# A hybrid decoder layer on one core: the attention stage with TensorE's instructions in a written-out order

## The chip, the core and the metric

The kernel runs on one core of a Trainium2 chip. A core has five engines with an instruction stream each: TensorE (PE in the profile; its weight loads are shown as PEld), VectorE (DVE), ScalarE (ACT), GpSimd (POOL) and SyncE (SP), which here only issues transfers. Each stream is fixed when the kernel is built; an engine takes its instructions in that order, and an instruction whose semaphore isn't set yet holds up all that stand behind it on its engine. Matmuls write to PSUM, eight banks of 128 x 512 floats; everything else lives in SBUF. The metric is the time of one execution on the device in microseconds (us), the median of the runs.

## The reference, cut to what matters

One decoder layer on x of 512 tokens x 1024, in float32:

```
proj = x @ w_in                       # q, k, v, forget logits, z, xBC, dt, two gates
log_f = log_sigmoid(f_logit + b_forget)
attn: 16 heads of 64; logit[t,s] = q_t.k_s / 8 + sum_{s<j<=t} log_f_j, causal softmax, times v
ssm:  Mamba-2 SSD, 32 heads of 64 in 4 groups, state 128, chunks of 128, gated RMS norm
mixed = (g0 * (attn @ w_proj_attn) + g1 * (ssm @ w_proj_ssm)) @ w_out    # g = sigmoid(gate + b)
x = layer_norm(a * x + mixed)
x = layer_norm(a * x + (silu(x @ w_ffn_gate) * (x @ w_ffn_up)) @ w_ffn_down)
```

## The kernel before, in words

Every large product is made of three matmuls on operands that are split into a high and a low part (`mm3`, lines 135 to 137), each with up to 512 moving columns. A weight chunk of 128 x 1024 comes in by one transfer on SP's queue (`load_w`), and `split` makes its two parts: ScalarE copies the high one (line 101), VectorE subtracts the low one (line 102). There are four buffers for raw chunks and three for each part.

Two helpers make projections. `gemm_ws` holds weights still: 256 output rows in two PSUM banks (tag `gps`, four banks), eight weight blocks of 128, so 16 times `mm3` for the usual 1024 inner rows, or 48 matmuls; then `evac` empties each bank. `gemm_xs` holds the tokens still: 512 output columns in four `gps` banks, 32 times `mm3`.

The stages are: the transposed x; for four groups the SSD branch (`group_bc`, `group_x`, `group_z`, `group_y`, `group_u`, `group_proj`); attention; the two gate projections; the attention output projection; `w_out` and the first layer norm; a feed-forward part; the second layer norm.

In attention, `att_qk(hg, isq, qk)` projects q or k of four heads. Its evacuation makes two tiles per head: ScalarE copies (line 397), VectorE copies and subtracts (lines 398 and 399), GpSimd sets ones and issues a small transfer of the forget sums. These tiles have two buffers per tag, so those of one group of four heads come free as that group's scores are done. `att_v(hg)` projects v of eight heads. `att_head` then does one head:

- scores: for each of four query blocks two matmuls of 128, 256, 384 or 512 columns into one bank (tag `cps`, four banks; lines 426 and 427);
- softmax of each block: VectorE masks and takes the maximum (line 431), ScalarE takes the exponential (line 433), VectorE the reciprocal (line 434) and the scaling (line 435) of a tile `t_y`;
- ten 128 x 128 transposes (line 448) into three `cps` banks, each split by ScalarE and VectorE into high and low tiles (`t_uh`, `t_ul`, `t_sq`, `t_xw`);
- PV: eight matmuls into a `cps` bank (line 454), whose two halves ScalarE (line 458) and VectorE (line 459) add up.

The order on each engine is set when the kernel is built: a scheduler takes the instructions by the order in which the program writes them, with estimated times, and issues on each engine the first that is ready. So TensorE's order around a head is the scheduler's: the projections that are written later (the next group's q and k, then the second gate's `evac_g1`, lines 650 to 660) stand between the parts of a head as filler. Weight splits have a higher priority.

Of the kernel before, what the change touches and what calls it, by code (L numbers as in the profile page):

```python
# [1 line left out]

# [9 lines left out]
AF = mybir.ActivationFunctionType  # L13
ALU = mybir.AluOpType
# [4 lines left out]
T = 512  # L19
NT = T // P  # L20
# [20 lines left out]
def tile_hybrid_decoder_layer(  # L41
# [58 lines left out]
    def split(hi, lo, src):  # L100
        nc.scalar.copy(out=hi, in_=src)  # L101
        nc.vector.tensor_tensor(out=lo, in0=src, in1=hi.bitcast(F32), op=ALU.subtract)  # L102

    def gps():
        return psum.tile([P, T], F32, name="gps", bufs=4)

    def cps():
        return psum.tile([P, T], F32, name="cps", bufs=4)
# [7 lines left out]
    def slot(tag, shape=(P, T), dtype=F32):  # L116
        return HOME.get(tag, sbb).tile(list(shape), dtype, name="t_" + tag, tag=tag, bufs=BUFS[tag])

    def big(tag, a=4, dtype=F32):
        return slot(tag, (P, a, 2048 // a), dtype)  # L120
# [13 lines left out]
    def mm3(o, l, r, start, stop, skip=False):  # L134
        nc.tensor.matmul(out=o, lhsT=l[0], rhs=r[0], start=start, stop=False, skip_group_check=skip)  # L135
        nc.tensor.matmul(out=o, lhsT=l[0], rhs=r[1], start=False, stop=False, skip_group_check=skip)  # L136
        nc.tensor.matmul(out=o, lhsT=l[1], rhs=r[0], start=False, stop=stop, skip_group_check=skip)  # L137
# [1 line left out]
    def ws_chunk(w, c0, half, dst=None):  # L139
        return load_w(w[half * 512:(half + 1) * 512, c0:c0 + 256], 4, 256, dst)  # L140

    def gemm_ws(w, c0, nk, rhs, evac, alloc=gps, n=T, chunks=None):

        ps = [alloc()[:, 0:n] for _ in range(2)]
        for half in range(nk // 4):
            hi, lo = chunks[half] if chunks else ws_chunk(w, c0, half)
            for b in range(2):
                bs = slice(b * P, (b + 1) * P)
                for k in range(4):
                    kt = half * 4 + k  # L150
                    mm3(ps[b], (hi[k][:, bs], lo[k][:, bs]), rhs(kt), kt == 0, kt == nk - 1)
        for b in range(2):
            evac(b, ps[b])

    def gemm_xs(w, c0, lhs, evac, before=None):

        ps = [gps() for _ in range(NT)]
        for kc in range(KD // 2):
            hi, lo = load_w(w[kc * 256:(kc + 1) * 256, c0:c0 + T], 2, T)
            for tt in range(NT):  # L160
                if before is not None and kc == 0:
                    before(tt)
                for k in range(2):
                    kt = kc * 2 + k
                    mm3(ps[tt], lhs(kt, tt), (hi[k], lo[k]), kt == 0, kt == KD - 1)
                if kc == KD // 2 - 1:
                    evac(tt, ps[tt])

    def down_chunk(w, kc, half, dst=None):
        return load_w(w[kc * 256:(kc + 1) * 256, half * T:(half + 1) * T], 2, T, dst)  # L170
# [208 lines left out]
    QK = (("v", "th", "bT", "cT"), ("btok", "cbm", "xst", "xdt"))  # L379

    def att_qk(hg, isq, qk):
        c0 = (C_Q if isq else C_K) + hg * 256
        sc = 0.125 if isq else 1.0

        def evac(b, ps):
            for par in range(2):
                h = hg * 4 + 2 * b + par
                src = ps[par * 64:(par + 1) * 64, :]
                t1 = slot(QK[isq][2 * par], (68, T), F32R)
                t2 = slot(QK[isq][2 * par + 1], (P, T), F32R)  # L390
                a, l_ = (0, 64) if isq else (64, 0)
                nc.gpsimd.memset(t1[64:68, :].bitcast(F32), 1.0)
                if isq:
                    nc.gpsimd.dma_start(out=t1[64:66, :], in_=cuT[h:h + 33:32, :])
                else:
                    nc.gpsimd.dma_start(out=t1[66:68, :], in_=cuT[64 + h:97 + h:32, :])
                nc.scalar.activation(out=t1[0:64, :], in_=src, func=AF.Copy, scale=sc)
                nc.vector.tensor_copy(out=t2[a:a + 64, :], in_=t1[0:64, :].bitcast(F32))
                nc.vector.scalar_tensor_tensor(out=t2[l_:l_ + 64, :], in0=src, scalar=sc, in1=t1[0:64, :].bitcast(F32),
                                               op0=ALU.mult, op1=ALU.subtract)  # L400
                qk[(isq, h)] = (t1, t2)
        gemm_ws(w_in, c0, KD, rhs_x, evac)

    def att_v(hg):

        vt = [slot("xtok", (P, NT, 4, P), F32R) for _ in range(2)]

        def evac(tt, ps):
            sv = ps.rearrange("p (h d) -> p h d", h=8)
            for i in range(2):  # L410
                hi = vt[i][:, tt, :, 0:64]
                nc.scalar.copy(out=hi, in_=sv[:, 4 * i:4 * i + 4])
                nc.vector.tensor_tensor(out=vt[i][:, tt, :, 64:128], in0=sv[:, 4 * i:4 * i + 4], in1=hi.bitcast(F32), op=ALU.subtract)
        gemm_xs(w_in, C_V + hg * 256, lhs_x, evac)
        return vt

    def att_head(h, qk, vt, of):
        hh = h % 4
        q1, q2 = qk[(True, h)]
        k1, k2 = qk[(False, h)]  # L420
        pr = []
        for i in range(NT):
            n = (i + 1) * P
            qs = slice(i * P, (i + 1) * P)
            ps = cps()
            nc.tensor.matmul(out=ps[:, 0:n], lhsT=q1[:, qs], rhs=k1[:, 0:n], start=True, stop=False)  # L426
            nc.tensor.matmul(out=ps[:, 0:n], lhsT=q2[:, qs], rhs=k2[:, 0:n], start=False, stop=True)  # L427
            sm = cst0.tile([P, 3], F32, name="sm", bufs=6)
            pt = slot("y")

            nc.vector.tensor_tensor_reduce(out=pt[:, 0:n], in0=ps[:, 0:n], in1=mneg[:, T - n:T], scale=-1.0, scalar=-NEG,  # L431
                                           op0=ALU.add, op1=ALU.min, accum_out=sm[:, 2:3])
            nc.scalar.activation(out=pt[:, 0:n], in_=pt[:, 0:n], func=AF.Exp, scale=-1.0, bias=sm[:, 2:3], accum_out=sm[:, 0:1])  # L433
            nc.vector.reciprocal(out=sm[:, 1:2], in_=sm[:, 0:1])
            nc.vector.tensor_scalar(out=pt[:, 0:n], in0=pt[:, 0:n], scalar1=sm[:, 1:2], scalar2=None, op0=ALU.mult)
            pr.append(pt)
        ab = big("uh" if h % 2 == 0 else "ul", 4, F32R)
        cc = slot("sq" if h % 2 == 0 else "xw", (P, 2, 256), F32R)
        pT = {}
        for j, kbs in enumerate(((0,), (1, 3), (2,))):  # L440
            ps = cps()
            o = 0
            hi, lo = (ab[:, j, :], ab[:, 2 + j, :]) if j < 2 else (cc[:, 0, :], cc[:, 1, :])
            for kb in kbs:
                w = T - kb * P
                pT[kb] = (hi[:, o:o + w], lo[:, o:o + w])
                for i in range(kb, NT):
                    nc.tensor.transpose(out=ps[:, o:o + P], in_=pr[i][:, kb * P:(kb + 1) * P], identity=ident)  # L448
                    o += P
            split(hi[:, 0:o], lo[:, 0:o], ps[:, 0:o])  # L450
        po = cps()
        for kb in range(NT):
            for j in range(2):
                nc.tensor.matmul(out=po[:, kb * P:], lhsT=vt[:, kb, hh, :], rhs=pT[kb][j],  # L454
                                 start=kb == 0 and j == 0, stop=kb == NT - 1 and j == 1)
        rows = slice((h % 2) * 64, (h % 2 + 1) * 64)
        tb = slot("yo", (64, T))
        nc.scalar.copy(out=tb, in_=po[64:128, :])
        nc.vector.tensor_tensor(out=of[rows, :], in0=po[0:64, :], in1=tb, op=ALU.add)
# [152 lines left out]
    for g in range(NG):  # L612
# [10 lines left out]
        elif g < NG - 1:  # L623
            st = group_bc(g + 1)
            for pair in range(2):
                group_x(g + 1, st, pair)
    att_qk(0, True, qk)
    att_qk(0, False, qk)
    group_proj(NG - 1, u)


# [3 lines left out]
        oslots += [b_[:, i, :] for i in range(4)]  # L635
    oslots += [slot("ab", (P, T), F32R) for _ in range(6)]
    oT = [(oslots[2 * i], oslots[2 * i + 1]) for i in range(KD)]
    for hg in range(4):
        if hg > 0:
            att_qk(hg, True, qk)  # L640
            att_qk(hg, False, qk)
        if hg % 2 == 0:
            vts = att_v(hg)
        vt = vts[hg % 2]
        for h in range(4 * hg, 4 * hg + 4):
            if h % 2 == 0:
                of = slot("dx")
            att_head(h, qk, vt, of)
            if h % 2 == 1:
                split(oT[h // 2][0], oT[h // 2][1], of)  # L650


    for pair in range(4):
        def evac_g1(b, ps):
            j = 2 * pair + b
            th = slot("y")
            nc.scalar.activation(out=th, in_=ps, func=AF.Tanh, scale=0.5, bias=vec[:, 32 + j:33 + j])
            nc.vector.scalar_tensor_tensor(out=sd[j], in0=th, scalar=1.0, in1=sd[j], op0=ALU.add, op1=ALU.mult)
        gemm_ws(w_in, C_G + D + pair * 256, KD, rhs_x, evac_g1)
    g0 = {}  # L660
    for pair in range(4):
        def evac_g0(b, ps):
# [395 lines left out]
```

## Time and profile before

| | us |
|---|---|
| median of 3 runs (1150.43 to 1151.94) | 1150.79 |
| the profiled execution | 1153.12 |
| its span, first to last instruction | 1151.4 |
| TensorE busy in the span | 1121.1 (97%) |
| VectorE busy | 776.6 (67%) |
| ScalarE busy | 528.4 (46%) |
| GpSimd busy | 133.8 (12%) |

The profile's page gives the busy time of each engine and the span in 40 equal slices, a digit for the busy tenths of each slice. Other views ask the trace: windows (busy time of each engine in a stretch), the timeline (instructions in order of time: start, duration, engine, line, operation, output and inputs, shapes, count; idle time before it in brackets), waits (who waited for whom), and groups of instructions by line. Matmuls are pipelined and their ends are modelled; what one costs is read from the starts of neighbours. A few records of matmuls are missing. The attention stage lies from 461.7 us on, the first score matmul, to 644.5 us.

### The profile page before, as it was taken

Reading aid. Unit: us, or ns where it says so; the run is one execution under the profiler, and the core shown is the slowest. Engines: PE = TensorE matmul, PEld = TensorE weight load, DVE = VectorE, ACT = ScalarE, POOL = GpSimd, SP = SyncE. Lnnn points to the kernel's source line nnn. Section 1 sums busy time; section 2 is a strip of 40 time slices with the busy share of each in tenths; the row PEclk is TensorE's granted clock in tenths of the full one; section 3 lists DMA queues with packets and bytes.
Section 4 is the critical chain, followed back from the end, with each engine's and each line's share of the span. In section 5 each row is a group of like instructions: output and inputs, shape, how many; then the busy total and the mean of one; then the engine's idle time right before and its main releaser. Section 6 shows DMA issues by size and latency. Waiting matters only on the chain.

```text
span 1151.4 us, 15793 instructions
## 1 busy us (share of the span) xinstructions
PE 1121.1 (97%) x6086; PEld 942.4 (82%) x6086; DVE 776.6 (67%) x1219; ACT 528.4 (46%) x912; POOL 133.8 (12%) x165
## 2 busy tenths in 40 slices
PE   7999999999999999999999999999999999999996
PEld 5887778778787788777777888888999999988885
DVE  3679974884787563889598534556986877667326
ACT  3376664454542432666465444214654554452210
POOL 3003130030123100221110000020111111100001
PEclk9999999999999999999999999999999999999998
DMA  8343233233231233211212235381778786465211
GB/s 249 91 132 115 85 112 92 92 110 93 91 91 58 91 92 95 71 56 56 80 51 57 80 124 179 118 195 68 205 177 216 170 199 155 93 228 175 92 55 74
DMA packets 115772, 134.21 MB, mean 117 GB/s; under 512 B 5636, under 2 KB 93936, under 8 KB 115568
## 3 DMA queue, kind: packets, MB, share of 16 engines
q1 hardware_dynamic: 99328, 112.80, 31.6%
q0 software_dynamic: 14640, 14.10, 7.6%
q10 hardware_dynamic: 1728, 6.29, 1.5%
q8 instruction: 48, 0.79, 0.3%
q14 instruction: 28, 0.23, 0.1%
HBM read 128.78 MB, written 4.26 MB: 116 GB/s over the span
## 4 chain that ended last, share of the span: by engine, by line
PE 44%; DVE 3%; issue 3%; DMA 2%; ACT 1%; POOL 0%; DVEq 0%; POOLq 0%; ACTq 0%; SPq 0%
PE gps L135 9%; PE gps L136 9%; PE gps L137 9%; PE cps L136 5%; PE cps L137 5%; PE cps L135 5%; DMA rq<-in_w_ffn_up_dram 1%; PE cps L448 1%; PE cps L454 1%; DMA t_sd<-in_x_dram 0%; DVE xr L726 0%; PE cps L426 0%; DMA raw<-in_w_ffn_down_dram 0%; PE cps L427 0%; DVE wlo L102 0%
## 5 line engine op out<-in xcount | busy, mean ns | idle before, releaser
L102 DVE TENSOR_TENSOR wlo<-raw,whi 128x1024 fp32r<-128x1024 f32 x127 | 156.3, 1230 | 210.7 <-ACT whi L101 210.2
L101 ACT CAST whi<-raw 128x1024 fp32r<-128x1024 f32 x127 | 133.6, 1052 | 272.4 <-PE gps L137 109.5
L135 PE MATMUL gps<-xh,whi 128*128 128x512 f32 x456 | 181.6, 398 | 0.0
L136 PE MATMUL gps<-xl,whi 128*128 128x512 f32 x456 | 181.6, 398 | 0.0
L137 PE MATMUL gps<-xh,wlo 128*128 128x512 f32 x456 | 181.3, 398 | 0.0
L101 ACT CAST wh<-rq 128x1024 fp32r<-128x1024 f32 (+1 forms) x84 | 82.2, 980 | 101.0 <-PE cps L136 44.9
L102 DVE TENSOR_TENSOR wl<-rq,wh 128x1024 fp32r<-128x1024 f32 (+1 forms) x84 | 94.9, 1132 | 33.8 <-ACT wh L101 33.7
L135 PEld LDWEIGHTS gps<-xh,whi 128*128 128x128 f32 x456 | 86.2, 189 | 16.5 <-issue 0.2
L136 PEld LDWEIGHTS gps<-xl,whi 128*128 128x128 f32 x456 | 86.2, 189 | 16.1 <-issue 0.2
L137 PEld LDWEIGHTS gps<-xh,wlo 128*128 128x128 f32 x456 | 86.2, 189 | 15.5
L135 PE MATMUL gps<-whi,xh 128*128 128x512 f32 x192 | 76.2, 397 | 3.8 <-ACT xh L101 3.7
L137 PE MATMUL gps<-whi,xl 128*128 128x512 f32 x192 | 75.8, 395 | 0.0
L136 PE MATMUL gps<-wlo,xh 128*128 128x512 f32 x192 | 75.7, 394 | 0.0
L233 DVE SCALAR_TENSOR_TENSOR t_v<-gps,cw,t_v 128x511 f32<-128x511 f32 (+2 forms) x72 | 53.4, 744 | 3.9 <-ACT t_v L230 3.1
L136 PE MATMUL gps<-t_ul,whi 128*128 128x512 f32 x128 | 51.1, 399 | 0.0
L137 PE MATMUL gps<-t_uh,wlo 128*128 128x512 f32 x128 | 51.0, 399 | 0.0
L135 PE MATMUL gps<-t_uh,whi 128*128 128x512 f32 x128 | 50.5, 395 | 0.0
L135 PEld LDWEIGHTS gps<-whi,xh 128*128 128x128 f32 x192 | 36.6, 190 | 12.3 <-ACT xh L101 4.4
L433 ACT ACTIVATE t_y<-t_y,sm 128x128 f32<-128x128 f32 (+1 forms) x64 | 35.8, 561 | 19.3 <-DVE sm L431 17.7
L315 ACT ACTIVATE t_ab<-t_ab,acum 128x128 f32<-128x128 f32 x128 | 41.8, 393 | 4.9 <-DMA t_ab<-ac_d 4.7
L784 POOL DMA_DIRECT2D rq<-in_w_ffn_gate_dram x12 | 15.5, 1296 | 244.6 <-ACT xh L686 158.7
L136 PEld LDWEIGHTS gps<-wlo,xh 128*128 128x128 f32 x192 | 36.6, 191 | 8.0 <-DVE wlo L102 0.5
(567 smaller groups left out, 2762.0 us busy)
## 6 DMA issues: line engine op xcount, KB each, us to landing
raw<-in_w_in_dram SPq DMA_DIRECT2D x80, 512.0 KB, 3.6
rq<-in_w_ffn_gate_dram SPq DMA_DIRECT2D x25, 512.0 KB, 4.7
rq<-in_w_ffn_up_dram SPq DMA_DIRECT2D x25, 512.0 KB, 5.3
raw<-in_w_ffn_down_dram SPq DMA_DIRECT2D x22, 512.0 KB, 3.8
t_ab<-ac_d SPq DMA_DIRECT2D x32, 256.0 KB, 3.3
raw<-in_w_proj_ssm_dram SPq DMA_DIRECT2D x16, 512.0 KB, 3.4
rq<-in_w_ffn_gate_dram POOLq DMA_DIRECT2D x10, 512.0 KB, 7.0
rq<-in_w_ffn_up_dram POOLq DMA_DIRECT2D x10, 512.0 KB, 6.1
```

What stands on the lines that cost most here:

```text
L101: nc.scalar.copy(out=hi, in_=src)
L102: nc.vector.tensor_tensor(out=lo, in0=src, in1=hi.bitcast(F32), op=ALU.subtract)
L135: nc.tensor.matmul(out=o, lhsT=l[0], rhs=r[0], start=start, stop=False, skip_group_check=skip)
L136: nc.tensor.matmul(out=o, lhsT=l[0], rhs=r[1], start=False, stop=False, skip_group_check=skip)
L137: nc.tensor.matmul(out=o, lhsT=l[1], rhs=r[0], start=False, stop=stop, skip_group_check=skip)
L233: nc.vector.scalar_tensor_tensor(out=v[:, sh:], in0=ps[:, 0:T - sh], scalar=cw[:, k, blk:blk + 1], in1=v[:, sh:], op0=ALU.mult, op1=ALU.add)
L315: nc.scalar.activation(out=m[:, r, :], in_=m[:, r, :], func=AF.Relu, scale=-1.0, bias=acum[:, c, h:h + 1])
L433: nc.scalar.activation(out=pt[:, 0:n], in_=pt[:, 0:n], func=AF.Exp, scale=-1.0, bias=sm[:, 2:3], accum_out=sm[:, 0:1])
L448: nc.tensor.transpose(out=ps[:, o:o + P], in_=pr[i][:, kb * P:(kb + 1) * P], identity=ident)
L454: nc.tensor.matmul(out=po[:, kb * P:], lhsT=vt[:, kb, hh, :], rhs=pT[kb][j], start=kb == 0 and j == 0, stop=kb == NT - 1 and j == 1)
L784: nc.gpsimd.dma_start(out=self.v(t), in_=self.q(*s_), accum_op=ALU.add)
```

## The change

`gemm_ws` becomes a generator, `ws_steps`, that hands control back after each `mm3`; `gemm_ws` runs it to its end. The evacuation of a bank is now written right behind that bank's last matmul. `xs_steps` is the same for the v projection. `att_head` falls into three functions: `att_scores` (scores and softmax), `att_transposes`, `att_values` (PV). The main loop of attention is written inside `tc.manual_schedule(engines={PE})`: there TensorE's instructions stand in the order in which the program writes them; the other engines keep the scheduler. Head h is: some filler steps, PV of head h-1, the ten transposes of head h, some more filler, the scores of head h+1. `before_t` and `after_t` count the filler for each head. Through head 7 the filler is q and k of groups 1 and 2 (64 steps); then v of the upper eight heads (32 steps), q and k of group 3 (32) and the second gate (64). The second gate's tanh is written back into its PSUM bank instead of a `t_y` buffer.

```diff
-    def gemm_ws(w, c0, nk, rhs, evac, alloc=gps, n=T, chunks=None):
+    def gemm_ws(*args):
+        for _ in ws_steps(*args):
+            pass
+
+    def ws_steps(w, c0, nk, rhs, evac, alloc=gps, n=T, chunks=None):
...
                     mm3(ps[b], (hi[k][:, bs], lo[k][:, bs]), rhs(kt), kt == 0, kt == nk - 1)
-        for b in range(2):
-            evac(b, ps[b])
+                    if half == nk // 4 - 1 and k == 3:
+                        evac(b, ps[b])
+                    yield
...
+    def xs_steps(w, c0, lhs, evac):
+        ps = [gps() for _ in range(NT)]
+        for kc in range(KD // 2):
+            hi, lo = load_w(w[kc * 256:(kc + 1) * 256, c0:c0 + T], 2, T)
+            for tt in range(NT):
+                for k in range(2):
+                    kt = kc * 2 + k
+                    mm3(ps[tt], lhs(kt, tt), (hi[k], lo[k]), kt == 0, kt == KD - 1)
+                    if kt == KD - 1:
+                        evac(tt, ps[tt])
+                    yield
...
-    for hg in range(4):
-        if hg > 0:
-            att_qk(hg, True, qk)
-            att_qk(hg, False, qk)
-        if hg % 2 == 0:
-            vts = att_v(hg)
-        vt = vts[hg % 2]
-        for h in range(4 * hg, 4 * hg + 4):
-            if h % 2 == 0:
-                of = slot("dx")
-            att_head(h, qk, vt, of)
-            if h % 2 == 1:
-                split(oT[h // 2][0], oT[h // 2][1], of)
-
-    for pair in range(4):
-        def evac_g1(b, ps):
-            j = 2 * pair + b
-            th = slot("y")
-            nc.scalar.activation(out=th, in_=ps, func=AF.Tanh, scale=0.5, bias=vec[:, 32 + j:33 + j])
-            nc.vector.scalar_tensor_tensor(out=sd[j], in0=th, scalar=1.0, in1=sd[j], op0=ALU.add, op1=ALU.mult)
-        gemm_ws(w_in, C_G + D + pair * 256, KD, rhs_x, evac_g1)
+    def gates1():
+        for pair in range(4):
+            def evac_g1(b, ps, pair=pair):
+                j = 2 * pair + b
+                nc.scalar.activation(out=ps, in_=ps, func=AF.Tanh, scale=0.5, bias=vec[:, 32 + j:33 + j])
+                nc.vector.scalar_tensor_tensor(out=sd[j], in0=ps, scalar=1.0, in1=sd[j], op0=ALU.add, op1=ALU.mult)
+            yield from ws_steps(w_in, C_G + D + pair * 256, KD, rhs_x, evac_g1)
+
+    with tc.manual_schedule(engines={mybir.EngineType.PE}):
+        vts, steps = att_v(0)
+        for _ in steps:
+            pass
+        of = {}
+
+        def finish(h, pT):
+            if h % 2 == 0:
+                of[0] = slot("dx")
+            att_values(h, pT, vts[(h // 4) % 2], of[0])
+            if h % 2 == 1:
+                split(oT[h // 2][0], oT[h // 2][1], of[0])
+
+        def fill(n):
+            for _ in range(n):
+                if next(steps, 0) == 0:
+                    break
+
+        pr, pT = att_scores(0, qk), None
+        steps = chain(*(att_qk(hg, isq, qk) for hg in (1, 2) for isq in (True, False)))
+        before_t = {3: 5, 6: 6, 7: 1, 8: 16, 9: 10, 10: 10, 11: 12}
+        after_t = {3: 3, 6: 1, 7: 3, 8: 4, 11: 3}
+        for h in range(AH):
+            fill(before_t.get(h, 7))
+            if pT is not None:
+                finish(h - 1, pT)
+            pT = att_transposes(h, pr)
+            fill(after_t.get(h, 2))
+            if h == 7:
+                finish(h, pT)
+                pT = None
+                vts, steps = att_v(2)
+                steps = chain(steps, *(att_qk(3, isq, qk) for isq in (True, False)), gates1())
+                fill(8)
+            if h < AH - 1:
+                pr = att_scores(h + 1, qk)
+        finish(AH - 1, pT)
+        for _ in steps:
+            pass
```

## Rows read from the trace of the kernel before

**Rows 1.** The page, part 2: 40 slices of the span, busy tenths and clock of TensorE.
```profile
PE   7999999999999999999999999999999999999996
...
PEclk9999999999999999999999999999999999999998
```
**Rows 2.** Windows: stretch, length, busy us (instructions) of PE, PEld, DVE, ACT, POOL; clock, DMA.
```profile
461.70:543.00 81.30, 80.31 (x411) 62.03 (x410) 72.26 (x202) 54.01 (x125) 16.67 (x32) 1.00 0.19 56
543.00:562.90 19.90, 19.89 (x88) 15.96 (x88) 9.70 (x15) 6.64 (x11) 0.00 (x0) 1.00 0.31 93
562.90:644.50 81.60, 81.19 (x416) 62.93 (x416) 69.25 (x195) 53.13 (x123) 8.37 (x16) 1.00 0.21 59
```
**Rows 3.** Timeline of TensorE, fourteen dense projection matmuls up to the scores of head 8.
```profile
559.78 0.39 PE L136 MATMUL gps<-wlo,xh 128*128 128x512 f32 x1
...
562.73 0.39 PE L137 MATMUL gps<-whi,xl 128*128 128x512 f32 x1
562.96 0.22 PE L426 MATMUL cps<-t_v,t_btok 68*128 68x128 f32 x1
```
**Rows 4.** Timeline of TensorE, 596 to 613 us: transposes of two heads.
```profile
596.81 0.40 PE L137 MATMUL gps<-xh,wlo 128*128 128x512 f32 x1
597.21 0.55 PE L448 MATMUL cps<-ident,t_y 128*128 128x128 f32 x3
...
597.83 0.40 PE L136 MATMUL gps<-xl,whi 128*128 128x512 f32 x1
...
604.02 0.40 PE L135 MATMUL gps<-xh,whi 128*128 128x512 f32 x1
...
610.19 0.40 PE L135 MATMUL gps<-xh,whi 128*128 128x512 f32 x1
610.43 0.49 PE L448 MATMUL cps<-ident,t_y 128*128 128x128 f32 x3
...
610.99 0.39 PE L137 MATMUL gps<-xh,wlo 128*128 128x512 f32 x1
...
611.65 0.66 PE L448 MATMUL cps<-ident,t_y 128*128 128x128 f32 x4
...
612.65 0.50 PE L454 MATMUL cps<-t_uh,t_xtok 128*128 128x512 f32 x1
```
**Rows 5.** Waits of TensorE's weight loads, 461.7 to 644.5: us in total, times, longest.
```profile
PEld cps L448 <- DVE t_y L435: 11.5, 37, 0.8
PEld cps L454 <- ACT t_uh L101: 2.5, 8, 0.3
...
PEld cps L426 <- DVE sm L431: 2.3, 5, 0.6
```
**Rows 6.** Timeline of TensorE, the first projection matmul behind a score block.
```profile
481.77 0.40 PE L136 MATMUL gps<-xl,whi 128*128 128x512 f32 x1
```
**Rows 7.** Timeline of VectorE, the softmax behind that score block.
```profile
481.52 0.68 DVE L459 TENSOR_TENSOR t_dx<-cps,t_yo 64x512 f32<-64x512 f32 x1
...
482.98 0.68 DVE L102 TENSOR_TENSOR t_hn<-t_dx,t_hn 128x512 fp32r<-128x512 f32 x1
...
484.25 1.22 DVE L102 TENSOR_TENSOR wlo<-raw,whi 128x1024 fp32r<-128x1024 f32 x1
...
486.31 0.80 DVE L435 TENSOR_SCALAR t_y<-t_y,sm 128x384 f32<-128x384 f32 x2
487.14 0.69 DVE L399 SCALAR_TENSOR_TENSOR t_cbm<-gps,t_btok 64x512 fp32r<-64x512 f32 x1
```
**Rows 8.** Timeline of VectorE, the last split behind the four transposes of 611.65.
```profile
614.18 0.42 DVE L102 TENSOR_TENSOR t_sq<-cps,t_sq 128x256 fp32r<-128x256 f32 x1
```
**Rows 9.** Line 279, the SSD branch's transposes, and TensorE's idle time before them.
```profile
L279 PE MATMUL cps<-ident,t_xst x64: 270/273/303, 77.2 to 341.9; 128*128 128x128 f32 x64
...
  DVE t_xst L240: 0.2, 1
```

More of the change, by code (lines that the diff above doesn't have):

```diff
@@ L2 @@
 from contextlib import ExitStack
+from itertools import chain
 import concourse.bass as bass
@@ L401, in evac @@
                 qk[(isq, h)] = (t1, t2)
-        gemm_ws(w_in, c0, KD, rhs_x, evac)
+        return ws_steps(w_in, c0, KD, rhs_x, evac)
     def att_v(hg):
@@ L413, in evac, with att_scores @@
                 nc.vector.tensor_tensor(out=vt[i][:, tt, :, 64:128], in0=sv[:, 4 * i:4 * i + 4], in1=hi.bitcast(F32), op=ALU.subtract)
[L414 to L418, printed above, removed]
+        return vt, xs_steps(w_in, C_V + hg * 256, lhs_x, evac)
+    def att_scores(h, qk):
         q1, q2 = qk[(True, h)]
@@ L436, in att_head, with att_transposes @@
             pr.append(pt)
+        return pr
+    def att_transposes(h, pr):
         ab = big("uh" if h % 2 == 0 else "ul", 4, F32R)
@@ L450, in att_head, with att_values @@
             split(hi[:, 0:o], lo[:, 0:o], ps[:, 0:o])
+        return pT
+    def att_values(h, pT, vt, of):
+        hh = h % 4
         po = cps()
@@ L626, in tile_hybrid_decoder_layer @@
                 group_x(g + 1, st, pair)
-    att_qk(0, True, qk)
-    att_qk(0, False, qk)
+    for isq in (True, False):
+        for _ in att_qk(0, isq, qk):
+            pass
     group_proj(NG - 1, u)
@@ L646, in tile_hybrid_decoder_layer @@
+    with tc.manual_schedule(engines={mybir.EngineType.PE}):
[4 more added lines that the diff above has]
+        def finish(h, pT):
             if h % 2 == 0:
-                of = slot("dx")
-            att_head(h, qk, vt, of)
+                of[0] = slot("dx")
+            att_values(h, pT, vts[(h // 4) % 2], of[0])
             if h % 2 == 1:
-                split(oT[h // 2][0], oT[h // 2][1], of)
-    for pair in range(4):
-        def evac_g1(b, ps):
-            j = 2 * pair + b
-            th = slot("y")
-            nc.scalar.activation(out=th, in_=ps, func=AF.Tanh, scale=0.5, bias=vec[:, 32 + j:33 + j])
-            nc.vector.scalar_tensor_tensor(out=sd[j], in0=th, scalar=1.0, in1=sd[j], op0=ALU.add, op1=ALU.mult)
-        gemm_ws(w_in, C_G + D + pair * 256, KD, rhs_x, evac_g1)
+                split(oT[h // 2][0], oT[h // 2][1], of[0])
[23 more added lines that the diff above has]
+        for _ in steps:
+            pass
```

## The prediction

> **What bounds the kernel now.** I read the slices first. TensorE's digit is 9 in nearly every slice at full clock [rows 1], so idle time as such says little: what counts is how far apart the starts of neighbouring matmuls lie. Second, the windows around attention [rows 2]: heads 0 to 7 take 81.3 us, the v projection of the upper heads 19.9 us with little beside it, heads 8 to 15 81.6 us. TensorE is busy throughout, but VectorE is busy for 72.3 and 69.3 us of the two head stretches, 89% and 85%: it is the engine next to the bound. Third, the timeline, for prices.
>
> A dense projection matmul of 512 columns costs (562.96 - 559.78) / 14 = 0.227 us [rows 3]. At that rate a head's scores, 2 x (128 + 256 + 384 + 512) columns, cost 1.14 us, and its PV, which has the same columns, 1.14 us. Three transposes between two projections, not waited for, take 610.99 - 610.19 - 2 x 0.227 = 0.35 us, or 0.115 each [rows 4], so ten cost 1.15. A head is then 3.43 us of its own, eight heads 27.4.
>
> The first head stretch holds 411 matmuls [rows 2], of which 8 x 26 = 208 are the heads' and 203 projections: 203 x 0.227 + 27.4 = 73.5 us, against 81.3 that it took. The second: 208 projections, 47.2 + 27.4 = 74.6 against 81.6. So 7.8 + 7.0 = 14.8 us are lost there (a few missing records would make that smaller). That is the most that any other order of the same work can win.
>
> Where it goes: the list of waits [rows 5] has 37 weight loads waiting for a scaled softmax tile, 8 for the first split of a transpose alone, 5 for a score tile's buffers. The price of such a wait is seen by holding two like places side by side [rows 4]: the transposes of 597.21, which were waited for, stretch their neighbours' distance to 597.83 - 596.81 = 1.02 us; those of 610.43 left it at 0.80. So a wait costs 0.22 us even where the engine hardly stood idle; 50 of them are 11 us of the 14.8. The reason for so many is the order: each head's four softmax blocks are transposed one at a time as they come, and PV follows 1.0 us behind the last transposes (611.65 to 612.65 [rows 4]), while the splits that it reads end at 614.60 [rows 8].
>
> **The change, part by part.** *Grouping as such.* Unwaited transposes between projections cost 0.115 each, already less than a half projection's time apiece, and the projection behind them no more than its share. So putting ten in one block saves nothing by itself; I take 0, and what can be saved is the waits.
>
> [...]
>
> *Waits removed.* A head's transposes wait once at most instead of up to four times. PV of head h now comes after the scores of h+1 and 7 + 2 filler steps (about 9 x 3 x 0.227 = 6.1 us), where the splits need 614.60 - 611.65 = 2.95 us from the last transposes on [rows 4, 8]: PV's waits go, save at heads 7 and 15, which have only 3 and 2 steps (2.0 and 1.4 us) in between.
>
> *Waits added.* The order is now rigid. First, the ten transposes of head h wait for all four softmax blocks. Between the end of the scores and the block lie 7 steps (4.8 us) and PV (1.1): 5.9 us. Before, softmax took 487.11 - 481.77 = 5.3 us in one head [rows 6, 7], of which 0.68 + 0.68 + 1.22 = 2.6 us was other VectorE work between its steps, so bare it needs some 2.7; in another the last transposes came 611.65 - 604.02 = 7.6 us behind the scores [rows 4]. So it fits when VectorE is free and doesn't when projections' evacuations stand ahead. Queued behind a waiting block are the 2 filler steps, then the next scores, and all of softmax behind those. Second, the scores need four `cps` banks, which are PV's and the three of the transposes; the last is free when the last split is done, 2.95 us behind; the fourth score block comes about 1.15 x 0.4 + 1.4 + 0.7 = 2.5 us behind that point in the new order. So a small wait is likely there in busy heads. Third, head 7 has one step and PV between its scores and its transposes, 0.68 + 1.14 = 1.8 us: a stall of 0.9 us at least (2.7 bare), 5.8 at most (by the 7.6); I take 1.2, nearer to the bare end, since VectorE works on during it.
>
> *Heads 0 to 7.* The filler is 64 steps = 192 matmuls, 43.6 us; with 27.4 of the heads 71.0 us. The work was the same before but for 11 matmuls of v (2.5 us): 81.3 - 2.5 = 78.8 us. VectorE's work, 72.3 us, is unchanged and now the longer of the two. So here VectorE is late next. At best the stretch takes 72.3 + 1.2; at worst, with the 7.6 us softmax in every head, 71 + 7 x (7.6 - 5.9 - 0.35 of transposes that go first + 0.22) + 5.8, or 87.8. I take 4 us of VectorE idleness (9 before) plus the 1.2: 77.5, nearer to the lower end because before it also ran at 89% with a chain in each head that the new order breaks. Gain 1.3 us, bounds +5.3 and -9.0.
>
> *Heads 8 to 15.* 8 + 76 + 19 = 103 steps stand in them, 309 matmuls, 70.1 + 27.4 = 97.5 us, while VectorE's work is about 69.3 + 9.7 = 79 us [rows 2], 81%. TensorE bounds, and there is room for softmax: 16, 10, 10 and 12 steps before the first transposes. Of the 7.0 us I leave one wait of 0.22 per head and 0.13 for the scores' banks, 8 x 0.35 = 2.8: gain 4.2, bounds 6.5 and 0.
>
> *Other edits.* The 25 steps of the second gate that are left follow at the end as dense matmuls, as before: 0. Weight loads on SP's queue keep their number and nearly their order, with the DMA engines at 19 to 21% in the head stretches [rows 2]: 0, and the four raw buffers cover it; without them a chunk would have to land within 8 steps, 5.4 us. GpSimd's memsets and small transfers move with the q and k evacuations, which it does in 16.7 of 81.3 us [rows 2]: 0; if late they would hold up scores two or more heads on. Tanh written to PSUM has no row; it is eight ScalarE instructions with ScalarE two thirds busy, nothing waits but a bank two projections on: 0, between -0.3 and +0.5. The evacuation of a bank is also written earlier in every `gemm_ws`, the SSD branch's too. Its 64 transposes let TensorE idle for only 0.2 us on VectorE [rows 9], so its order hardly hangs on this: 0, at 16 evacuations and one wait each between -3.5 and +3.5.
>
> Sum: 1.3 + 4.2 = 5.5 us less. The span would be 1151.4 - 5.5 = 1145.9, the profiled execution 1153.1 - 5.5 = 1147.6. The profiled one stands 2.3 above the median of the runs, so the median would be 1150.8 - 5.5 = **1145.3 us**.
>
> **The rivals.** *All waits go.* VectorE keeps up in the lower heads and almost nothing is left in the upper: 5.3 + 6.2 = 11.5 us, 1139.3. For it: softmax bare is 2.7 us against 5.9 of room. Against: 72.3 us of VectorE work in 71 of TensorE's.
>
> *No change.* The waits move to other instructions: one block's wait is long where four were short. The order was fixed before too, and it is only another fixed order. For it: VectorE's 89%. Against: PV's waits have a clear cover. 1150.8, give or take 2.3.
>
> *Slower.* Place: the transposes of heads 0 to 7. Behind them TensorE can't take filler as it could before, when it did a block's transposes as each came. With VectorE's stream holding q and k evacuations ahead of the last softmax steps, as at 485 us where a weight split did so [rows 7], each block stands. It decides where the mean stall per head passes (78.8 + 4.2 - 71.0) / 8 = 1.5 us. At 1.9, near the 7.6 us case with its wait and head 7, the lower heads take 71 + 8 x 1.9 = 86.2, 7.4 more, and the upper gain 4: 1154.2.
>
> **How the numbers follow.** This kernel's runs tell apart about 0.2%, 2.3 us: faster is below 1148.5, slower above 1153.1. Chances: the forecast 0.50 (its own range 1142.5 to 1148.5), all waits go 0.20, no change 0.15, slower 0.15. That is 0.70 faster, 0.15 same, 0.15 slower. The range runs from 1138.5, just below the best case, to 1152.5, past most of the no-change case; some 0.05 lies below it and 0.15 above.
>
> **What would show it.** Waits for `t_y` should fall from 37 towards 16, those of line 454 to a few; the lower heads should take about 77.5 us with VectorE above 92%, the upper heads with their 103 steps about 100.3. If the lower heads take over 83 us with long idle times before line 448, the slower case holds. If line 426 waits for splits (line 102) in most heads, the banks were mis-sized. A change in the SSD stretch before 400 us would contradict the zero given there.

## The result and the profile after

The changed kernel takes 1163.14 us (1161.47 to 1163.17, five runs) against 1150.79 beside it, a ratio of 1.0096 with a 95% interval of 1.0082 to 1.011: it is slower by some 11 us by that ratio, 12.4 between the medians. The profiled execution took 1163.16 us, its span 1161.4. The prediction, 1145.3 in a range of 1138.5 to 1152.5, was wrong in its sign.

The page of the kernel after, parts 1 and 2, next to [rows 1]:

```profile
PE 1122.5 (97%) x6086; PEld 954.5 (82%) x6086; DVE 776.0 (67%) x1219; ACT 526.4 (45%) x912; POOL 133.1 (11%) x165
...
PE   7999999999999999998999999999999999999996
...
PEclk9999999999999999989999999999999999999998
```

The same number of instructions on each engine, and busy times within 2% of those before, but one slice each, between 490 and 555 us, in which TensorE is less busy (the 19th) and its clock lower (the 18th). The windows answer to [rows 2]; the first runs from the first scores of head 0 to those of head 8, the second on to those of head 15:

```profile
460.80:555.60 94.80, 87.13 (x425) 71.68 (x424) 76.26 (x208) 55.26 (x128) 16.38 (x32) 0.95 0.18 52
555.60:642.10 86.50, 84.38 (x433) 71.54 (x432) 65.74 (x178) 51.50 (x116) 8.07 (x16) 1.00 0.24 68
```

Heads 0 to 7 stand out: 94.8 us with TensorE busy for 87.1 and a mean clock of 0.95. To lay the kernels side by side I take each head from the start of its first score matmul to that of the next head's, count its matmuls, and subtract their prices as the prediction had them (0.227 us for 512 columns and in proportion, 0.115 for a transpose). What is left is the excess, in us; head 15 runs on to the first matmul of the attention output projection. The whole stage has the same 1184 matmuls in both:

```
head        0    1    2    3    4    5    6    7    8    9   10   11   12   13   14   15   sum
before    0.6  1.1  1.1  1.3  1.1  0.9  0.8  1.6  0.6  1.2  1.1  1.3  1.1  0.6  0.7  0.7  15.8
after     0.4  0.4  1.0  2.3  5.2  0.9  0.2  8.0  0.1  0.2  0.2  1.4  2.1  0.9  0.2  0.9  24.5
```

In seven of the heads the new order does what it was forecast to do: 0.1 to 0.4 us in place of 0.6 to 1.2. Heads 3 and 4, head 7, and heads 11 and 12 spoil it. The stage gives back 24.5 - 15.8 = 8.7 us of the 10.0 by which the span grew. The stretch ahead of it is 0.9 us shorter, the one behind it 2.2 longer.

The waits of TensorE's weight loads in attention, next to [rows 5]:

```profile
PEld cps L469 <- DVE t_y L453: 4.6, 5, 1.6
PEld cps L444 <- DVE t_ul L103: 4.0, 5, 1.6
PEld cps L444 <- DVE t_sq L103: 3.8, 6, 0.6
...
PEld cps L479 <- ACT t_xst L417: 0.4, 1, 0.4
```

Line 469 is the transposes, 444 the scores, 479 PV. Waits for softmax fell from 37 to 5, PV's to one. But scores now wait for splits, and the few waits are long. Head 4's scores, in the timeline of TensorE (the wait of 1.00 us ahead of the first of them is counted in head 3):

```profile
499.97 0.40 PE L138 MATMUL gps<-xh,wlo 128*128 128x512 f32 x1
501.37 0.30 PE L444 MATMUL cps<-t_v,t_btok 68*128 68x128 f32 x1 [1.00 <-issue]
...
503.80 0.69 PE L444 MATMUL cps<-t_v,t_btok 68*128 68x384 f32 x1 [1.38 <-DVE t_ul L103]
...
505.46 0.63 PE L136 MATMUL gps<-xh,whi 128*128 128x512 f32 x1
505.89 0.63 PE L137 MATMUL gps<-xl,whi 128*128 128x512 f32 x1
```

What VectorE did meanwhile:

```profile
499.55 0.42 DVE L418 CAST t_th<-t_v 64x512 fp32r<-64x512 f32 x1
499.99 0.68 DVE L419 SCALAR_TENSOR_TENSOR t_th<-gps,t_v 64x512 fp32r<-64x512 f32 x1
500.59 0.67 DVE L484 TENSOR_TENSOR t_dx<-cps,t_yo 64x512 f32<-64x512 f32 x1
501.19 0.67 DVE L103 TENSOR_TENSOR t_ul<-cps,t_ul 128x512 fp32r<-128x512 f32 x1
501.89 0.42 DVE L418 CAST t_cT<-t_bT 64x512 fp32r<-64x512 f32 x1
502.33 0.69 DVE L419 SCALAR_TENSOR_TENSOR t_cT<-gps,t_bT 64x512 fp32r<-64x512 f32 x1
503.06 0.69 DVE L103 TENSOR_TENSOR t_ul<-cps,t_ul 128x512 fp32r<-128x512 f32 x1
```

It evacuates k of heads 4 to 7 (`t_th`, `t_cT`), four pairs that start between 496.1 and 501.9 us, because the fill ahead of head 3's transposes brings both banks of that projection to their ends within five steps. The add of the PV before (line 484), which ends at 501.26 just ahead of the first score matmul, and the splits that free the other score banks stand among them. Behind it the matmuls start 505.89 - 505.46 = 0.43 us apart, where 0.227 is usual; the windows (clock third from the right) say why:

```profile
500.00:503.00 3.00, 1.28 (x6) 0.59 (x4) 2.96 (x5) 0.59 (x1) 0.00 (x0) 1.00 0.43 156
503.00:506.50 3.50, 2.70 (x7) 2.31 (x8) 3.04 (x13) 1.70 (x7) 1.14 (x3) 0.51 0.00 0
506.50:510.00 3.50, 3.50 (x10) 2.73 (x9) 1.49 (x7) 0.81 (x2) 0.99 (x2) 0.51 0.02 2
510.00:513.00 3.00, 3.00 (x15) 2.44 (x15) 0.96 (x1) 1.05 (x1) 0.00 (x0) 1.00 0.02 5
```

TensorE was busy for 1.28 of 3.0 us, and then its clock stood at half for nearly 7 us, 0.51 in both of the next windows, most of which it worked without a pause; from 510 us on it is 1.00 again. At head 7 the same follows a stall at the transposes, with the clock at 0.53, 0.50 and 0.50 in the three microseconds from 544 to 547 us:

```profile
541.32 0.33 PE L469 MATMUL cps<-ident,t_y 128*128 128x128 f32 x1 [1.44 <-DVE t_y L453]
542.82 0.33 PE L469 MATMUL cps<-ident,t_y 128*128 128x128 f32 x1 [1.17 <-DVE t_y L453]
543.80 0.33 PE L469 MATMUL cps<-ident,t_y 128*128 128x128 f32 x1 [0.65 <-DVE t_y L453]
544.39 1.76 PE L469 MATMUL cps<-ident,t_y 128*128 128x128 f32 x7 [0.26 <-DVE t_y L453]
545.80 0.78 PE L136 MATMUL gps<-xh,whi 128*128 128x512 f32 x1
546.38 0.63 PE L137 MATMUL gps<-xl,whi 128*128 128x512 f32 x1
```

VectorE again, with k and q of heads 8 to 11 (line 418 and line 419) between this head's maxima (line 449) and its scalings:

```profile
537.99 0.27 DVE L449 CUSTOM_DVE_ANT_0 t_y<-cps,mneg 128x128 f32<-128x128 f32 x1
...
538.20 0.59 DVE L418 CAST t_xdt<-t_xst 64x512 fp32r<-64x512 f32 x1
538.80 0.69 DVE L419 SCALAR_TENSOR_TENSOR t_xdt<-gps,t_xst 64x512 fp32r<-64x512 f32 x1
539.41 0.41 DVE L418 CAST t_cT<-t_bT 64x512 fp32r<-64x512 f32 x1
539.84 0.69 DVE L419 SCALAR_TENSOR_TENSOR t_cT<-gps,t_bT 64x512 fp32r<-64x512 f32 x1
...
540.63 0.43 DVE L449 CUSTOM_DVE_ANT_0 t_y<-cps,mneg 128x256 f32<-128x256 f32 x1
```

The step counts don't explain q's pair (`t_xdt`) at this place: `t_xst`, from which it is made, is q of head 11, whose matmuls were done by 521 us. Its buffer is that of head 7's own q, so GpSimd's memset and ScalarE's copy into it start where head 7's scores end:

```profile
537.53 0.52 POOL L412 MEMSET t_xst<- 4x512 f32 x1 [7.63 <-PE cps L444]
```
```profile
537.54 0.59 ACT L417 ACTIVATE t_xst<-gps 64x512 fp32r<-64x512 f32 x1 [1.25 <-issue]
538.10 0.59 ACT L417 ACTIVATE t_bT<-gps 64x512 fp32r<-64x512 f32 x1
```

The copy of k (`t_bT`) stands behind it on ScalarE. With two buffers per tag, then, the last q of the next group comes free for evacuation just when the fourth head's softmax begins; heads 3 and 11 have the same memset, at 492.4 and 597.7 us.

In attention the clock is low for 6.8 + 3.4 = 10.2 us. TensorE still waited for nearly 1 of them; the other 9.3 cost about 9.3 x (0.43 - 0.227) / 0.43 = 4.4 us. The heads that lost by the change lost 13.1 us together (the others won 4.4), so a third of that is the clock; stalls and matmuls set apart by waits make the rest.

### The profile page after: what moved, and what is told of

It is laid out like the page before. It is cut to its first block, busy times and chain, and to the rows that moved or that the text cites. A ratio compares the mean times of both kernels' runs of the same rounds, so it can differ in the third digit from the quotient of the medians.

```text
span 1161.4 us, 15817 instructions
## 1 busy us (share of the span) xinstructions
PE 1122.5 (97%) x6086; PEld 954.5 (82%) x6086; DVE 776.0 (67%) x1219; ACT 526.4 (45%) x912; POOL 133.1 (11%) x165
## 5 line engine op out<-in xcount | busy, mean ns | idle before, releaser
L136 PE MATMUL gps<-whi,xh 128*128 128x512 f32 x192 | 76.3, 397 | 3.8 <-ACT xh L102 3.8
```

## The experiments

The theory from the profile after: the loss sits in a few spots where VectorE is late for a TensorE that may not take other work. The rivals: a set order costs something everywhere; VectorE is simply full through head 7; the small edits are to blame. Each kernel ran beside the kernel before; the ratio is to that. All but the one with the small edits alone start from the changed kernel.

**Counts of head 7.**
```diff
-        before_t = {3: 5, 6: 6, 7: 1, 8: 16, 9: 10, 10: 10, 11: 12}
+        before_t = {3: 5, 4: 6, 5: 5, 6: 5, 7: 5, 8: 16, 9: 10, 10: 10, 11: 12}
```


> Edit: only the filler counts before the transposes change: heads 4, 5, 6 give 6, 5, 5 steps in place of 7, 7, 6 and head 7 gets 5 in place of 1. Theory (few spots): the loss sits in a few spots where VectorE is late, and behind the longer ones TensorE's clock stands at 0.50; head 7 is the largest, 8.0 us over the price of its matmuls. With 4 steps (2.7 us) more ahead of its transposes it falls to about 2 and the stretch of low clock at 544 us goes: 1157, give or take 2. Rival (a rigid order costs in every head, and VectorE is the bound through head 7): the wait only moves to heads 4 to 6, and the time stays at 1162 to 1164.


Measured 1158.65 us, ratio 1.0057 [1.0036, 1.0079]. Head 7's excess fell from 8.0 to 4.7, heads 5 and 6 rose from 1.1 to 2.3 together, and head 4 kept its 5.3 and its low clock. The stretch of low clock at head 7 stayed too (536.9 to 540.3). Head 7's transposes no longer wait; its scores do, once for 1.59 us, as head 4's did. The stage's excess fell only from 24.5 to 22.6, so that the time lies within the theory's range is partly luck: of the 4.5 us between the two profiles 2.0 lie behind the stage. Both hold in part: the spot matters, and some of its wait moves.

**Splits first.**
```diff
-            split(hi[:, 0:o], lo[:, 0:o], ps[:, 0:o])
+            with tc.high_priority():
+                split(hi[:, 0:o], lo[:, 0:o], ps[:, 0:o])
         return pT
```


> Edit: the splits of the transposes get high priority, so that VectorE and ScalarE do them before waiting q and k evacuations; TensorE's order stays. Theory (few spots): the scores of heads 4 and 12 wait for PSUM banks that those splits empty, behind four evacuations of k; with the splits first, head 4 loses its 2.5 us of idle time and the 6.8 us of low clock, head 12 its 1.4 us: 5 to 6 us less, 1157 to 1158, with head 7 as before. Rival (VectorE is full, and its order doesn't matter): what is done later makes softmax late, 1161 to 1164.


Measured 1159.29 us, ratio 1.0073 [1.0058, 1.0088]. TensorE's order is unchanged, and head 4 falls from 5.2 to 1.2 us with full clock: its stall was VectorE's order. But head 5 rises by 1.0, head 7 to 8.9 and head 12 to 3.7, both with low clock behind them. The windows show head 4's stretch at full clock and head 12's at half:

```profile
489.30:522.70 33.40, 29.70 (x157) 24.95 (x156) 29.87 (x82) 20.66 (x48) 6.28 (x12) 1.00 0.20 59
```
```profile
610.00:613.00 3.00, 3.00 (x8) 2.32 (x8) 2.68 (x12) 1.93 (x7) 0.00 (x0) 0.50 0.00 0
```

The work put off is late elsewhere: the rival's part again.

**Bank by bank.** `att_qk` runs the two banks of a projection one after the other:
```diff
+    def bank_steps(w, c0, rhs, evac):
...
+        for b in range(2):
+            bs = slice(b * P, (b + 1) * P)
+            for half in range(2):
+                if b == 0:
+                    parts[half] = ws_chunk(w, c0, half)
...
-        return ws_steps(w_in, c0, KD, rhs_x, evac)
+        return bank_steps(w_in, c0, rhs_x, evac)
```


> Edit: q and k projections finish one bank (eight steps) before the other starts, so their two evacuations lie eight steps apart and not four; TensorE does the same matmuls, counts unchanged. Theory (few spots): evacuations no longer pile up at the fourth head of a group; the excess of heads 3, 4, 11 and 12 falls from 11 to about 5 us, that of head 7, whose k comes 4 steps earlier, from 8 to about 5: 1154 to 1157. Rival (VectorE is full): same work on VectorE, 1161 to 1164.


Measured 1157.85 us, ratio 1.0056 [1.0035, 1.0077]. Heads 3, 4, 11 and 12 fell from 11.0 to 8.6, not to 5; head 7 from 8.0 to 4.7; head 1 rose from 0.4 to 2.1. Spreading the bursts helps, and doesn't settle it.

**The order left free.**
```diff
-    with tc.manual_schedule(engines={mybir.EngineType.PE}):
+    if True:
```


> Edit: the new program order without the set order on TensorE: the scheduler orders TensorE again, from the same text. Rival (rigidity): the scheduler moves projections into the stalls and the time comes back to 1151 or less. Theory (few spots): the scheduler follows the written order nearly everywhere, as its estimates see no stall at heads 4 and 7, and the time stays within 3 us of 1163.


Measured 1149.37 us, ratio 0.9982 [0.9971, 0.9992]. Here I was wrong. The builder does follow the written order nearly everywhere, but not at those spots, as the timeline of TensorE around head 4's scores shows:

```profile
501.89 0.39 PE L138 MATMUL gps<-xh,wlo 128*128 128x512 f32 x1
502.83 0.30 PE L444 MATMUL cps<-t_v,t_btok 68*128 68x128 f32 x1 [0.56 <-issue]
502.96 0.28 PE L445 MATMUL cps<-t_th,t_cbm 128*128 128x128 f32 x1
503.08 0.44 PE L136 MATMUL gps<-xh,whi 128*128 128x512 f32 x1
503.38 0.38 PE L444 MATMUL cps<-t_v,t_btok 68*128 68x256 f32 x1
503.60 0.28 PE L445 MATMUL cps<-t_th,t_cbm 128*128 128x256 f32 x1
503.72 0.39 PE L137 MATMUL gps<-xl,whi 128*128 128x512 f32 x1
...
505.26 0.44 PE L444 MATMUL cps<-t_v,t_btok 68*128 68x384 f32 x1
```

Three projection matmuls are taken ahead of these scores, one between the first pairs and six where the kernel after stood for 1.38 us; head 7's transposes are taken in ones, twos, threes and fours again. The stage's excess is 13.0 us, 0.8 in head 4 and 1.8 in head 7, at a clock of 1.00 from 462.2 to 632.3 us. So, by one profile of each, the written order alone is worth 15.8 - 13.0 = 2.8 us in the stage, and forbidding the scheduler to leave it costs 24.5 - 13.0 = 11.5.

**Gate steps early.** If VectorE's load per filler step is what makes the set order fail, lighter filler should mend it. Half of the second gate, which otherwise comes in or behind the upper heads, goes into the lower ones:
```diff
-        steps = chain(*(att_qk(hg, isq, qk) for hg in (1, 2) for isq in (True, False)))
-        before_t = {3: 5, 6: 6, 7: 1, 8: 16, 9: 10, 10: 10, 11: 12}
-        after_t = {3: 3, 6: 1, 7: 3, 8: 4, 11: 3}
+        g1 = gates1()
+        steps = chain(*(chain(islice(g1, 16), att_qk(hg, True, qk), att_qk(hg, False, qk)) for hg in (1, 2)))
+        before_t = {0: 9, 1: 9, 2: 9, 3: 9, 4: 9, 5: 9, 6: 9, 7: 9, 8: 14, 9: 10, 10: 10, 11: 12}
+        after_t = {0: 3, 1: 3, 2: 3, 3: 3, 4: 3, 5: 3, 6: 3, 7: 3, 11: 3}
...
-                steps = chain(steps, *(att_qk(3, isq, qk) for isq in (True, False)), gates1())
+                steps = chain(steps, *(att_qk(3, isq, qk) for isq in (True, False)), g1)
```


> Edit: set order as in the changed kernel, but 32 of the second gate's 64 steps, which ask little of VectorE, stand in heads 0 to 7 (a gate pair ahead of q and k of each group): 9 steps before and 3 after the transposes of each head there, in place of 7 and 2; heads 8 to 11 get 14, 10, 10, 12 before, and 2, 2, 2, 3 after. Theory now (a rigid order is good where VectorE has room, and costs stalls plus low clock where its work per filler step is too dense): the excess over the matmuls' prices in heads 0 to 7 falls from 18.3 to about 6 us, no low clock inside attention: 1147 to 1151. Rival (a set order costs in itself, because the builder's free order was 14 us better with the same text): 1155 or more.


Measured 1147.81 us, ratio 0.996 [0.9946, 0.9975]. Heads 0 to 7 have 4.6 us of excess in place of 18.4, and no low clock: the time came as the theory had it, and the excess, expected at about 6, below it. In the kernel after, VectorE was busy for 76.3 us beside matmuls that price at 94.8 - 18.4 = 76.4, so it had no room at all; here it is 84.1 beside 98.2. The edit also puts more steps between scores and transposes, in head 7 nine in place of one, and no run separates this from the lighter load.

**Gate steps early, bank by bank.**


> Edit: the gate steps early and the q and k projections bank by bank. Theory: evacuations spread as well; 0 to 2 us below the kernel with gate steps early alone, 1146 to 1150. Rival (set order costs in itself): 1154 or more.


Measured 1144.78 us, ratio 0.9931 [0.9915, 0.9948]: 7 us faster than the kernel before, and 3.0 below gate steps early alone, where 0 to 2 were expected; the stage accounts for 10.7 - 8.8 = 1.9 of them. The windows, heads 0 to 7 and 8 to 14, and the waits of weight loads (lines 461 and 496 are scores and PV here):

```profile
460.30:561.40 101.10, 100.80 (x521) 85.87 (x520) 84.26 (x216) 62.92 (x136) 16.25 (x32) 1.00 0.25 70
561.40:644.40 83.00, 81.61 (x421) 69.19 (x420) 65.38 (x177) 49.76 (x115) 8.09 (x16) 1.00 0.24 65
```
```profile
PEld cps L461 <- DVE t_sq L103: 2.7, 5, 0.6
...
PEld cps L461 <- DVE t_ul L103: 0.6, 2, 0.3
```

The first window holds 32 gate steps more than that of the kernel after, which price at 32 x 3 x 0.227 = 21.8 us, at 6.3 us more. VectorE is busy for 84.3 of 101.1 us, 83%. Seven of the eight lower heads lie between 0.1 and 0.7 us of excess; what is left in the list is the scores waiting for splits, mostly in the upper heads, and two waits of PV of 0.7 and 0.6 us.

**Gate steps early, order free.**


> Edit: the same text as with gate steps early, TensorE's order left to the scheduler. Theory (room on VectorE makes the set order harmless): within 2 us of the set one, 1146 to 1151. Rival (set order costs in itself): 5 us or more below the set one.


Measured 1145.65 us, ratio 0.9944 [0.9929, 0.9959], an excess of 9.5 in the stage against 10.7 with the order set: 2.2 us below it, where the theory allowed 2 and the rival asked for 5. The runs hardly overlap (1145.27 to 1147.15 against 1146.88 to 1148.88), so where VectorE has room a set order may still cost some 2 us, not 11, and wins nothing over the scheduler's. The stage accounts for 1.2 of the 2.2.

**The small edits alone**, on the kernel before:
```diff
-        for b in range(2):
-            evac(b, ps[b])
+                    if half == nk // 4 - 1 and k == 3:
+                        evac(b, ps[b])
...
-            nc.scalar.activation(out=th, in_=ps, func=AF.Tanh, scale=0.5, bias=vec[:, 32 + j:33 + j])
+            nc.scalar.activation(out=ps, in_=ps, func=AF.Tanh, scale=0.5, bias=vec[:, 32 + j:33 + j])
```


> Edit: the kernel before with only the two small edits of the change: each bank's evacuation written right behind its last matmul, and the second gate's tanh written into its PSUM bank. Theory: they are worth nothing, within 2 us of the kernel before. Rival (they carry a part of the loss, or of the gain with a free order): 2 us or more off.


Measured 1151.69 us, ratio 0.9997 [0.9988, 1.0006], and the stage's excess is 15.9. They are worth nothing that this interval, some 1 us either way, can tell.

**A third step behind the transposes**, on top of gate steps early and bank by bank:
```diff
+        before_t = {8: 13, 9: 11, 10: 9, 11: 11, 12: 5, 13: 5, 14: 5, 15: 5}
+        after_t = {}
...
-            fill(before_t.get(h, 7))
+            fill(before_t.get(h, 9))
...
-            fill(after_t.get(h, 2))
+            fill(after_t.get(h, 3))
```


> Edit: gate steps early and q and k bank by bank, and in heads 8 to 15 three filler steps behind the transposes in place of two (13, 11, 9, 11 and four times 5 before them). Theory: what is left in the upper heads are the scores' waits for the last split, 0.31 us each with a bubble, and head 9's PV waiting for v; a third step covers them: 2 to 3 us less than with two, so 1142 to 1144 where the other gave 1144.8. Rival (softmax needs those steps ahead of the transposes): the waits move to line 469 and nothing is won or up to 5 us are lost.


Measured 1144.84 us (1142.71 to 1148.38), ratio 0.994 [0.9925, 0.9955]: no better than with two, within its spread. Heads 9, 13 and 15 fell to 0.4, 0.2 and 0.4 us from 1.0, 0.9 and 1.4, but head 11 rose from 0.9 to 1.4 and head 12 from 1.0 to 2.1, where the transposes now wait twice, 0.5 and 1.0 us, as the rival had it. The stage's excess is 8.2 against 8.8: small, and nothing won in the time.

## Why the prediction was wrong, point by point

*Where the time was lost before.* Right. The excess per head by this measure is 0.6 to 1.6 us, and heads whose waits are gone run at 0.1 to 0.4.

*Grouping as such, 0; the small edits, 0.* Right: the block of ten transposes adds nothing in unstalled heads (0.1 to 0.4 us of excess), and the run with the small edits alone stands at 0.9997. The order of the SSD branch gave no loss either.

*Waits removed.* Right: 37 became 5, and PV waits once.

*Waits added: the scores' banks.* The mechanism was named, its size wrong: "a small wait is likely there in busy heads", 0.13 us per head. In the plain heads it is 0.31 us of idling and, with the matmuls around it set apart, some 0.7 us of excess (0.9 in head 13 against 0.2 in head 14, which has no such wait). At head 4 it is the largest stall but one, 1.0 + 1.38 us of idling. I bounded it by the time the splits need on a VectorE that is free for them [rows 8] and didn't look at what the step counts bring to VectorE just there: both banks of k end within the five steps ahead of head 3's transposes. Counting steps against evacuations would have shown it. The sign that was named for mis-sized banks came: scores (line 444 now) wait for splits 16 times, in nine of the heads.

*Head 7.* Taken at 1.2 us, at most 5.8; its excess is 8.0, stalls and low clock together. The 1.8 us of room was right. The end that I chose was not: the softmax took from 537.5, the end of the scores, to 544.3, nearly as long as in the slow head of [rows 4], since three pairs of evacuations came between, one of them held back by head 7's own scores. That the tiles' two buffers would release an evacuation just there stood in no term. "VectorE works on during it" was no reason for the lower end; that work was the stall's cause.

*The clock.* No term of the sum, no rival. 10.2 us at half clock cost some 4.4. The profile before had an example in the idle last slice, busy for 6 tenths at a clock of 8 tenths [rows 1], and another in its windows, 0.50 from 64 to 66 us, and I read "full clock" as a property of the stage, where it was one of a stage whose longest listed wait was 0.8 us [rows 5].

*Heads 0 to 7 at 77.5 us.* They took 94.8 with eight steps of v more, which are 5.4: 89.4, past even the bound of 87.8, which held no clock. *Heads 8 to 15: gain 4.2.* The excess went from 7.3 to 6.1, a gain of 1.2; heads 11 and 12, with 3.5 between them, hold the rest, and for the same cause as 3 and 4.

*The sum and the rivals.* The failed step is the term for heads 0 to 7, 77.5 us by 4 us of VectorE idleness and 1.2 for head 7, where 89.4 were measured; it was chosen as "nearer to the lower end because before it also ran at 89% with a chain in each head that the new order breaks". At 89% the scheduler's order had been filling the times at which VectorE is late with projections; the free order with the new text shows that this filling, and not the chain, was worth the larger part. The slower rival had the right engine, the right reason (evacuations ahead of softmax) and a threshold of 1.5 us per head that was passed at 18.4 / 8 = 2.3, but not the place: it had each block of transposes stand, and the time went at heads 3, 4 and 7, in the first two at the scores. It had chance 0.15 and 1154.2, short by the scores' banks and the clock.

*Behind the stage.* The remaining 2.2 us are hardly the change's order. In the layer norm TensorE idles for a like time in both kernels, and only in one does the clock fall behind it. Windows of the kernel before:

```profile
808.00:812.00 4.00, 2.43 (x19) 2.03 (x17) 4.00 (x5) 4.00 (x6) 1.31 (x1) 1.00 0.27 82
812.00:816.00 4.00, 3.91 (x33) 3.92 (x34) 4.00 (x6) 1.35 (x3) 0.02 (x1) 1.00 1.04 198
```

Windows of the kernel after:

```profile
816.00:820.00 4.00, 2.37 (x18) 1.96 (x17) 4.00 (x5) 4.00 (x5) 1.34 (x1) 1.00 0.31 85
820.00:824.00 4.00, 4.00 (x21) 4.00 (x22) 4.00 (x5) 0.22 (x1) 0.00 (x0) 0.57 1.04 186
```

From the first output projection matmul to the end it took 446.5 to 447.1 us in the four profiles (after, and the kernels with splits first, bank by bank, and the order free) whose clock fell there, and 444.8 to 445.4 in the seven where it didn't. The start of attention, too, moved between 458.8 and 462.2 us among profiles of nearly the same work. In seven of the eleven, those of before and after among them, the clock stood at half for 3.4 us from 62 or 63 us on, and attention starts at 460.1 to 462.2; in the four others it starts at 458.8 to 460.4. What decides where the clock falls was not tried.

## What to carry to other kernels

A written-out order takes from the scheduler the right to put other work where an engine would wait, worth 11.5 us in this stage, so it is safe only where each waiting instruction has its operands well before its turn: for every wait, count what the filler's own evacuations put on the engine that makes the operand, step by step, not on average, and look at which buffer each evacuation waits for. Put filler that is cheap for the engine next to the bound where that engine is full; here this, with the projections bank by bank, turned a loss of 11 us into a gain of 7. The gain is that of the new program text with this filler and not of setting the order: left free, the text with the gate steps early alone gave 6.6. And price a long stall with the clock behind it: the two at heads 4 and 7 cost 4.4 us in low clock beside 6.6 in idling.

## What the runs showed of the hardware

A wait at which TensorE hardly idled cost 0.22 us in matmuls set apart [rows 4]. The stalls at heads 4 and 7, with 2.5 and 4.1 us of idling, had half clock behind them for 6.8 and 3.4 us, which cost some 2.9 and 1.5 us more. The single stall of 1.4 us in head 12 left the clock alone in the kernel after; with splits first a stall of 1.3 us in the same head had 3.4 us of half clock behind it. In the layer norm, too, the clock fell behind nearly the same idle time (2.43 and 2.37 us busy of 4.0) in one profile and not in the other. So these runs give no idle time from which on the clock falls.
